# Two wide RWKV stages: VectorE's convolution taps placed behind the triangular inverse, and a new order of the filler work

## The chip, the cores and the metric

One core of one Trainium2 chip runs the whole program. The metric is device time in microseconds (us) for one execution, as the median of several runs. Engines are named as the profile names them: PE is TensorE, DVE is VectorE, ACT is ScalarE, POOL is GpSimd, SP is the queue that issues all loads.

## The reference, cut to what matters

Two blocks follow each other on 256 tokens of width 1024. The first has two layers. Each layer takes two token streams (`ctx` and `x`) through the following, cut to what the change touches:

```python
mod_x = silu_c @ ada_w[l] + ada_b[l]                      # adaLN: six shift, scale and gate rows
ux = modulate(rmsnorm(x, norm1_g[l]), sh1, sc1) @ w_in[l]  # "norm of x", then the input product
# first 1024 columns of ux: the convolution's input (value and gate); the rest: RWKV
z = val * sigmoid(gate)
z = dwconv(z, conv_w) + conv_b                             # 31 taps along the tokens, 512 channels
z = silu(group_norm(z, 8, cnorm_g, cnorm_b))
yx, s_f, s_b = rwkv_scans(prep, s0_f, s0_b)                # a recurrence over tokens in both directions
mix = concat([z, rwkv_out(yx)]);  x = x + gt1 * (mix @ w_out[l]);  then a SwiGLU
```

The second block (two layers of SwiGLU, mixer, SwiGLU) follows, and the change does not touch it.

## The kernel before, in words

Activations lie feature-major (features on the partitions, 256 tokens along the free side). A product in full precision is three matmuls of a split operand: every weight piece of 512 KB is loaded by SP into a tile `raw` (four buffers), ACT writes its high part `wh` (L341) and DVE its low part `wl` (L342), and PE runs 24 matmuls for one output of 128 features (`up`, L333 is the helper that records every matmul).

The recurrence is done in chunks of 64 tokens. For each chunk a unit triangular matrix is inverted. All of its 32x32 diagonal blocks are inverted at once by DVE: `inverse` runs 31 steps, each a multiplication (L961) and a subtraction (L963), and each step needs the one before. Beside it run `reads` (masks on DVE, L1028) and `values` (masks, L1064). Both need PE, and the inverse's result is needed by the last part, the `chain`: two groups of four steps in which small matmuls, DVE and ACT alternate. Between the chain's steps the program calls `fill(FILL)`, which takes up to six steps of a list of other work, the filler.

This arrangement, called `wide`, is used twice: for `ctx` in layer 0 (from about 100 us on) and for `x` in layer 1 (from about 1130 us on). In both its filler is the convolution's input product of the same stream (`conv_in`, 8 weight pieces) and then adaLN for four of the six rows (`ada_steps`, 32 loads of 512 KB, 16 steps). After the chain comes the depthwise convolution in program order (`conv`): of the 30 outer taps per channel group f (there are four), `NPOOL` or `NPOOLE` gives how many POOL multiplies (L731) and how many ACT multiplies (L729); POOL adds all of those products up (L732). The remaining taps and the middle one are DVE's (L718 and L725, into a tile `T1c` of two buffers), and L736 joins both sums. Products wait in `tap` tiles, of which there are two (`NTAP`).

In layer 0 the stage is followed by `conv_in` of `x`, then `w_in` of `x` (15 weight pieces), then the output product of `ctx`. The norm of `x` (`norm_x`: two loads, squares, 16 transposes L438, and 24 evictions into four tiles of the ring `S`) stands in program order after the chain. The convolution of `x` is then done by POOL alone in the background (`NPOOLC`).

The order of each engine's work is not the program's order. A planner keeps its own estimate of every instruction's cost, takes for each engine the earliest instruction in program order that is ready by that estimate, and so fills waiting time with later work. A tile must find a free buffer in its ring before its first writer is ready: `S` has 20 buffers, `z` 2, the PSUM ring `pb` 2 (the filler's products, the norm's transposes and adaLN all use `pb`). On the chip each engine then works through its list in that order. `issue_after(ins)` puts the instructions of its block behind `ins` on the same engine.

Of the kernel before, what the change touches and what calls it, by code (L numbers as in the profile page):

```python
# [12 lines left out]
ALU = mybir.AluOpType  # L13
# [21 lines left out]

NLAST = 2, 4

NPOOL, NPOOLE, NPOOLC = (14, 3), (12, 4), (30, 0)
NTAP = 2

QB, QE, QC, EVERY = (2, 3, 4, 5), (2, 3, 4, 5), (1,), 2

FILL = 6
LATER = 1500
# [214 lines left out]
class Prog:  # L259
# [440 lines left out]
    def conv(self, l, z, acc, npool, hold=False):  # L700


        nc = self.nc
        o = COLS[f"convw{l}"][0]
        taps = sorted((j for j in range(31) if j != 15), key=lambda j: abs(j - 15))
        nv, na = 30 - npool[0] - npool[1], npool[1]
        parts = [("v", taps[:nv]), ("a", taps[nv : nv + na]), ("p", taps[nv + na :])]

        order = []
        for k, js in parts:  # L710
            order += [((i + 0.5) / len(js), k, j) for i, j in enumerate(js)]
        order.sort()
        zc = [acc[:, f, :] for f in range(4)]
        for f in range(4):
            w = lambda j: self.cols[:, o + 4 * j + f : o + 4 * j + f + 1]
            av = self.T1([P, T]) if nv else None
            if nv:
                nc.vector.tensor_scalar(av, z[:, f, :], w(15), None, ALU.mult)  # L718
                nc.gpsimd.memset(zc[f], 0.0)
            else:  # L720
                nc.gpsimd.tensor_scalar(zc[f], z[:, f, :], w(15), None, ALU.mult)
            for i, (_, k, j) in enumerate(order):
                d, s = slice(max(0, 15 - j), min(T, T + 15 - j)), slice(max(0, j - 15), min(T, T + j - 15))
                if k == "v":
                    nc.vector.scalar_tensor_tensor(av[:, d], z[:, f, s], w(j), av[:, d], ALU.mult, ALU.add)  # L725
                else:
                    t = self.t(self.pool, [P, T], "tap", bufs=NTAP)
                    if k == "a":
                        nc.scalar.mul(t[:, d], z[:, f, s], w(j))  # L729
                    else:  # L730
                        nc.gpsimd.tensor_scalar(t[:, d], z[:, f, s], w(j), None, ALU.mult)  # L731
                    nc.gpsimd.tensor_add(zc[f][:, d], zc[f][:, d], t[:, d])  # L732
                if i % 5 == 4:
                    yield
            if nv:
                nc.vector.scalar_tensor_tensor(zc[f], av, self.col(f"convb{l}", f), zc[f], ALU.add, ALU.add)  # L736
            else:
                nc.gpsimd.tensor_scalar(zc[f], zc[f], self.col(f"convb{l}", f), None, ALU.add)
            yield
        while hold and not self.go:  # L740
            yield
        self.group_norm(zc, f"cng{l}", f"cnb{l}", LN_EPS, AF.Silu)
# [200 lines left out]
    def inverse(self, Ld, Lo):  # L943

        nc = self.nc
        fl = lambda t: t.rearrange("p d a c x -> p (d a c) x")
        Ld, Lo = fl(Ld), fl(Lo)  # L950
        tj = self.S([P, 32, 32])
        nc.vector.transpose(tj.rearrange("p r c -> p c r"), Ld.rearrange("p j c -> p c j"))
        X = self.S([P, 32, 32])
        nc.gpsimd.memset(X, 0.0)
        xf = X.rearrange("p r c -> p (r c)")
        nc.gpsimd.memset(xf[:, 0:1024:33], 1.0)
        for k in range(31):
            m = 31 - k
            tmp = self.T1([P, 256])
            tv = tmp[:, 0 : m * (k + 1)].rearrange("p (a b) -> p a b", b=k + 1)  # L960
            nc.vector.tensor_mul(tv, tj[:, k + 1 : 32, k : k + 1].broadcast_to([P, m, k + 1]),  # L961
                                 X[:, k : k + 1, 0 : k + 1].broadcast_to([P, m, k + 1]))
            nc.vector.tensor_sub(X[:, k + 1 : 32, 0 : k + 1], X[:, k + 1 : 32, 0 : k + 1], tv)  # L963
        yield
        qt = self.S([P, 32, 32])
        nc.vector.transpose(qt, X)
        qc = self.S([P, 32, 32])
        nc.vector.transpose(qc, X.rearrange("p r c -> p c r"))

        zss = []  # L970
        for d in range(2):
            pz = self.ps((P, 16, 32))
            zs = Lo[:, 16 * d : 16 * d + 16, :]
            for j in range(16):
                J = 16 * d + j
                for h in range(2):
                    r = slice(64 * h + 32, 64 * h + 64)
                    w = slice(64 * h, 64 * h + 32)
                    self.mm(pz[w, j, :], Lo[r, J, :], qt[r, :, J], tile_position=(64 * h + 32, 64 * h))
            for h in range(2):  # L980
                w = slice(64 * h, 64 * h + 32)
                (nc.scalar.copy if h else nc.vector.tensor_copy)(zs[w], pz[w])
            zss.append(zs)
        Q = [self.S([P, 16, CH]) for _ in range(2)]
        for d in range(2):
            nc.gpsimd.memset(Q[d], 0.0)
            js = slice(16 * d, 16 * d + 16)
            src, zs = (qt, qc)[d], zss[d]
            po = self.ps((P, 16, 32))
            for q in range(4):  # L990
                s = slice(32 * q, 32 * q + 32)
                o = (q % 2) * 32
                dst, v = Q[d][s, :, o : o + 32], src[s][:, :, js].rearrange("p c j -> p j c")
                (nc.vector.tensor_copy if q % 2 else nc.scalar.copy)(dst, v)
            for j in range(16):
                J = 16 * d + j
                for h in range(2):
                    w = slice(64 * h, 64 * h + 32)
                    r = slice(64 * h + 32, 64 * h + 64)
                    if d == 0:  # L1000
                        self.mm(po[w, j, :], qc[w, :, J], zs[w, j, :], tile_position=(64 * h, 64 * h))
                    else:
                        self.mm(po[r, j, :], zs[w, j, :], qc[w, :, J], tile_position=(64 * h, 64 * h + 32))
            for h in range(2):
                w = slice(64 * h + 32 * d, 64 * h + 32 * d + 32)
                dst = Q[d][w, :, 32 * (1 - d) : 32 * (1 - d) + 32]
                if h:
                    nc.scalar.mul(dst, po[w], -1.0)
                else:
                    nc.vector.tensor_scalar(dst, po[w], -1.0, None, ALU.mult)  # L1010
        self.Q = Q
# [399 lines left out]
    def first(self):  # L1411
        nc = self.nc
        self.setup()
        RW = list(range(NRW))
        KWV = [4, 5, 6, 7, 8, 9, 10, 11, 12]
        drain = lambda g: [None for _ in g]
# [4 lines left out]
        fl = lambda t: t.rearrange("p (a b) -> p a b", a=4)  # L1421
        z = lambda: self.t(self.pool, [P, 4, T], "z", bufs=2)

        def wide(l, x, s0, ada, perm, before=None):

            def filler():

                steps = itertools.chain(self.conv_in(l, x, fl(self.x[0])), self.ada_steps(l, ada))

                def fill(n=1):  # L1430
                    lane = self.lane
                    self.on("b")
                    for _ in range(n):
                        next(steps, None)
                    self.on(lane)

                return fill

            self.pstags = alone
            for at in self.rwkv(l, self.w_in(l, x, RW), s0, True, "wide", filler()):  # L1440
                if at == "post" and before is not None:
                    before()
            self.on("c")
            drain(self.conv(l, fl(self.x[0]), fl(self.x[1]), (NPOOL, NPOOLE)[l]))
            self.pstags = beside
            self.on("b")
            return self.mixed_in(fl(self.x[1]), self.y, perm)

        self.ada(0, (1, 0))
        cf = self.load("ctx")  # L1450
# [1 line left out]
        cf = self.norm1(0, cf, 1, False, self.xf)  # L1452
        early = []

        def norm_x():
            zt = lambda: self.t(self.pool, [P, D], "z", bufs=2)
            self.on("b")
            early.append(self.norm1(0, self.load("x", [zt(), zt()]), 0, False, self.Sr, keep=True))
            self.on("r")

        cm = wide(0, cf, None, QB, False, norm_x)
        states = self.states
        self.on("b")
        (xf,) = early
        zx = z()
        mods = self.ada_steps(0, [q for q in (2, 3, 4, 5) if q not in QB])
        for _ in self.conv_in(0, xf, zx):
            next(mods, None)
            next(mods, None)
        drain(mods)  # L1470
        win = self.w_in(0, xf, RW)
        ux = next(win)
        drain(win)
# [25 lines left out]
        for b in range(2):  # L1499
            nc.sync.dma_start(self.keep[b], self.x[b])  # L1500
        xf = self.norm1(1, self.x, 0, True, self.xf, acc=True)
        xm = wide(1, xf, states, QE, True)
        for b in range(2):
            nc.sync.dma_start(self.x[b], self.keep[b])
        f = self.out(1, self.x, 0, xm)
# [132 lines left out]
```

## Time and profile before

| | |
|---|---|
| three runs | 2772.6, 2772.72, 2775.5 us (median 2772.72) |
| the profiled execution | 2776.2 us, its span 2774.1 us |
| PE, PE weight load | busy 95% and 82% of the span |
| DVE, ACT, POOL | busy 62%, 48%, 24% |
| mean granted TensorE clock | 0.961 |

How to read it: the span runs from the first to the last instruction. PE is busy nearly always, but the granted clock, shown beside the busy time in the tables by stretch, has to be read with it: busy time at clock 0.50 does half the work of busy time at 1.00.

### The profile page before, as it was taken

The page shows a single profiled execution, that of the slowest core. Times are in us where ns is not written, and L with a number is a line of the kernel's source. Part 1 is how long each engine was busy: PE and PEld are TensorE (multiplying, and loading weights), DVE is VectorE, ACT ScalarE, POOL GpSimd, SP SyncE. Part 2 cuts the span into 40 slices and gives each one's busy share as a digit, 9 for nine tenths or more (in the row PEclk, how much of TensorE's full clock was granted, in tenths as well). Part 3 has the DMA queues.
Part 4 walks back from the last instruction along what each step waited for, and adds up shares of the span by engine and source line. Part 5 has one row for each costly group of instructions (what it writes and reads, how often), then busy time and mean ns, then how long its engine had stood idle before and what let it go on. Part 6 is the DMA issues. An engine that isn't in the chain of part 4 may idle for free.

```text
span 2774.1 us, 53770 instructions
## 1 busy us (share of the span) xinstructions
PE 2628.3 (95%) x22398; PEld 2288.3 (82%) x22398; DVE 1713.4 (62%) x2703; ACT 1327.6 (48%) x2015; POOL 667.0 (24%) x669
## 2 busy tenths in 40 slices
PE   7889988999889998899899899999999999999998
PEld 4866867888678897866799899889899898889897
DVE  3885778655577555984555655666655655755655
ACT  5533654434564346433544544654544544644543
POOL 0287999920130001384200000010000000100000
PEclk9989989999999999979899999999999999999999
DMA  7244424434323354234355555524555554525653
GB/s 251 102 153 167 153 86 167 139 129 145 137 77 115 130 181 148 100 138 153 124 188 183 198 184 188 188 86 157 183 186 186 183 186 172 170 85 183 205 185 119
DMA packets 118767, 430.70 MB, mean 155 GB/s; under 512 B 13174, under 2 KB 13686, under 8 KB 118524
## 3 DMA queue, kind: packets, MB, share of 16 engines
q1 hardware_dynamic: 118524, 427.28, 44.7%
q8 instruction: 175, 2.87, 0.4%
q14 instruction: 68, 0.56, 0.1%
HBM read 425.13 MB, written 2.10 MB: 154 GB/s over the span
## 4 chain that ended last, share of the span: by engine, by line
PE 76%; DVE 10%; POOL 5%; ACT 5%; issue 2%; DMA 2%; SPq 0%; ACTq 0%; POOLq 0%; DVEq 0%
PE pb L333 32%; PE acc L333 24%; PE ps L333 19%; POOL tap L731 3%; DVE wl L342 2%; POOL z L732 1%; DVE T1c L725 1%; DMA raw<-in_ada 1%; DVE S L963 1%; DVE T L961 1%; POOL x L732 1%; ACT wh L341 1%; PE acc L438 0%; DMA raw<-in_wr 0%; ACT L384 0%
## 5 line engine op out<-in xcount | busy, mean ns | idle before, releaser
L342 DVE TENSOR_TENSOR wl<-raw,wh 128x1024 fp32r<-128x1024 f32 (+1 forms) x654 | 814.5, 1249 | 621.6 <-ACT wh L341 390.9
L341 ACT CAST wh<-raw 128x1024 fp32r<-128x1024 f32 (+1 forms) x654 | 681.8, 1046 | 892.7 <-PE pb L333 349.8
L333 PE MATMUL pb<-xf,wh 128*128 128x256 f32 (+1 forms) x2560 | 488.1, 289 | 15.6 <-DVE T1b L588 5.2
L333 PE MATMUL pb<-S,wh 128*128 128x256 f32 x2560 | 490.9, 289 | 4.3 <-DVE S L462 1.8
L333 PEld LDWEIGHTS pb<-xf,wh 128*128 128x128 f32 (+1 forms) x2560 | 411.3, 195 | 29.7 <-DVE T1b L588 8.8
L333 PEld LDWEIGHTS pb<-S,wh 128*128 128x128 f32 x2560 | 407.7, 192 | 21.5 <-issue 11.7
L333 PE MATMUL ps<-S,wh 128*128 128x256 f32 x2048 | 390.6, 288 | 0.5 <-ACT S L460 0.4
L333 PE MATMUL pb<-xf,wl 128*128 128x256 f32 (+1 forms) x1280 | 372.8, 292 | 8.9 <-DVE wl L342 8.9
L365 POOL TENSOR_TENSOR wl<-raw,wh 128x1024 fp32r<-128x1024 f32 x22 | 52.1, 2379 | 1340.7 <-ACT wh L364 824.2
L333 PE MATMUL pb<-S,wl 128*128 128x256 f32 x1280 | 367.4, 287 | 2.1 <-DVE wl L342 2.1
L333 PEld LDWEIGHTS ps<-S,wh 128*128 128x128 f32 x2048 | 327.0, 192 | 9.4 <-issue 3.7
L333 PE MATMUL ps<-S,wl 128*128 128x256 f32 x1024 | 293.8, 287 | 0.6 <-DVE wl L342 0.6
L333 PEld LDWEIGHTS pb<-xf,wl 128*128 128x128 f32 (+1 forms) x1280 | 249.3, 195 | 16.9 <-DVE wl L342 11.7
L333 PEld LDWEIGHTS pb<-S,wl 128*128 128x128 f32 x1280 | 245.3, 192 | 7.0 <-issue 3.2
L333 PE MATMUL acc<-wh,T 128*128 128x512 f32 x704 | 206.3, 393 | 0.0
L333 PEld LDWEIGHTS ps<-S,wl 128*128 128x128 f32 x1024 | 196.7, 192 | 3.0 <-issue 1.5
L333 PE MATMUL acc<-wh,T1b 128*128 128x512 f32 x528 | 158.6, 399 | 3.5 <-ACT T1b L341 3.5
L731 POOL TENSOR_SCALAR tap<-z,cols 128x255 f32<-128x255 f32 (+14 forms) x120 | 154.4, 1295 | 0.0
L333 PEld LDWEIGHTS acc<-wh,T 128*128 128x128 f32 x704 | 127.0, 189 | 23.6
L731 POOL TENSOR_SCALAR tap<-x,cols 128x246 f32<-128x246 f32 (+6 forms) x104 | 112.9, 1093 | 46.1 <-DVE x L670 46.0
L333 PEld LDWEIGHTS acc<-wh,T1b 128*128 128x128 f32 x528 | 94.9, 190 | 22.3 <-ACT T1b L341 4.4
L333 PE MATMUL acc<-wl,T 128*128 128x512 f32 x352 | 113.3, 395 | 0.0
(445 smaller groups left out, 3956.7 us busy)
## 6 DMA issues: line engine op xcount, KB each, us to landing
raw<-in_fu SPq DMA_DIRECT2D x132, 512.0 KB, 3.2
raw<-in_ada SPq DMA_DIRECT2D x96, 512.0 KB, 4.2
raw<-in_pu SPq DMA_DIRECT2D x88, 512.0 KB, 4.3
raw<-in_qu SPq DMA_DIRECT2D x88, 512.0 KB, 4.2
raw<-in_fd SPq DMA_DIRECT2D x66, 512.0 KB, 3.2
raw<-in_wr SPq DMA_DIRECT2D x51, 512.0 KB, 3.9
raw<-in_pd SPq DMA_DIRECT2D x44, 512.0 KB, 4.3
raw<-in_qd SPq DMA_DIRECT2D x44, 512.0 KB, 4.3
```

What stands on the lines that cost most here:

```text
L333: return self.nc.tensor.matmul(out, lhsT, rhs, start=start, stop=stop, **kw)
L341: self.nc.scalar.copy(hi, src)
L342: self.nc.vector.tensor_sub(lo, src, hi.bitcast(F32))
L365: self.nc.gpsimd.tensor_sub(lo, r, hi.bitcast(F32))
L725: nc.vector.scalar_tensor_tensor(av[:, d], z[:, f, s], w(j), av[:, d], ALU.mult, ALU.add)
L731: nc.gpsimd.tensor_scalar(t[:, d], z[:, f, s], w(j), None, ALU.mult)
L732: nc.gpsimd.tensor_add(zc[f][:, d], zc[f][:, d], t[:, d])
L961: nc.vector.tensor_mul(tv, tj[:, k + 1 : 32, k : k + 1].broadcast_to([P, m, k + 1]), X[:, k : k + 1, 0 : k + 1].broadcast_to([P, m, k + 1]))
L963: nc.vector.tensor_sub(X[:, k + 1 : 32, 0 : k + 1], X[:, k + 1 : 32, 0 : k + 1], tv)
```

## The change

Three things. DVE's first instruction of each channel group's taps (L718) is put behind the last subtraction of the inverse; its other taps depend on it. In both wide stages four more taps per channel group become DVE's: layer 0 from 14 on POOL, 3 on ACT and 13 on DVE to 10, 3 and 17; layer 1 from 12, 4 and 14 to 9, 3 and 18. And in layer 0 the filler becomes: `conv_in` of `ctx`, the norm of `x`, then adaLN's steps with one `conv_in` step of `x` after every fourth; what is left is run right after the stage. In layer 1 the filler stays as it was.

```diff
-NPOOL, NPOOLE, NPOOLC = (14, 3), (12, 4), (30, 0)
+NPOOL, NPOOLE, NPOOLC = (10, 3), (9, 3), (30, 0)
...
             if nv:
-                nc.vector.tensor_scalar(av, z[:, f, :], w(15), None, ALU.mult)
+                with self.tc.issue_after(self.inverted.ins):
+                    nc.vector.tensor_scalar(av, z[:, f, :], w(15), None, ALU.mult)
                 nc.gpsimd.memset(zc[f], 0.0)
...
-            nc.vector.tensor_sub(X[:, k + 1 : 32, 0 : k + 1], X[:, k + 1 : 32, 0 : k + 1], tv)
+            self.inverted = nc.vector.tensor_sub(X[:, k + 1 : 32, 0 : k + 1], X[:, k + 1 : 32, 0 : k + 1], tv)
...
-        def wide(l, x, s0, ada, perm, before=None):
+        def wide(l, x, s0, steps, perm):
...
-                steps = itertools.chain(self.conv_in(l, x, fl(self.x[0])), self.ada_steps(l, ada))
+                all_ = itertools.chain(self.conv_in(l, x, fl(self.x[0])), steps)
...
-            for at in self.rwkv(l, self.w_in(l, x, RW), s0, True, "wide", filler()):
-                if at == "post" and before is not None:
-                    before()
+            drain(self.rwkv(l, self.w_in(l, x, RW), s0, True, "wide", filler()))
...
-        def norm_x():
+        def then_x():
+
             zt = lambda: self.t(self.pool, [P, D], "z", bufs=2)
-            self.on("b")
             early.append(self.norm1(0, self.load("x", [zt(), zt()]), 0, False, self.Sr, keep=True))
-            self.on("r")
-
-        cm = wide(0, cf, None, QB, False, norm_x)
+            yield
+            early.append(z())
+            mods, conv = self.ada_steps(0, (2, 3, 4, 5)), self.conv_in(0, *early)
+            for i, _ in enumerate(mods):
+                yield
+                if i % 4 == 1:
+                    next(conv, None)
+                    yield
+            yield from conv
+
+        steps = then_x()
+        cm = wide(0, cf, None, steps, False)
+        drain(steps)
         states = self.states
         self.on("b")
-        (xf,) = early
-        zx = z()
-        mods = self.ada_steps(0, [q for q in (2, 3, 4, 5) if q not in QB])
-        for _ in self.conv_in(0, xf, zx):
-            next(mods, None)
-            next(mods, None)
-        drain(mods)
+        xf, zx = early
...
-        xm = wide(1, xf, states, QE, True)
+        xm = wide(1, xf, states, self.ada_steps(1, (2, 3, 4, 5)), True)
```

## Rows read from the trace of the kernel before

**Rows 1.** The page: busy time by engine, and the costliest group on DVE

```profile
PE 2628.3 (95%) x22398; PEld 2288.3 (82%) x22398; DVE 1713.4 (62%) x2703; ACT 1327.6 (48%) x2015; POOL 667.0 (24%) x669
...
L342 DVE TENSOR_TENSOR wl<-raw,wh 128x1024 fp32r<-128x1024 f32 (+1 forms) x654 | 814.5, 1249 | 621.6 <-ACT wh L341 390.9
```

**Rows 2.** Stretches of both wide stages: length, busy of each engine, clock, DMA

```profile
133.00:187.40 54.40, 46.89 (x465) 32.88 (x466) 52.43 (x112) 14.29 (x25) 45.80 (x45) 0.92 0.48 165
187.40:262.00 74.60, 73.44 (x1103) 51.28 (x1101) 42.07 (x80) 28.27 (x52) 58.58 (x69) 0.83 0.47 164
262.00:310.00 48.00, 47.58 (x329) 37.48 (x330) 29.45 (x51) 28.18 (x43) 44.05 (x48) 1.00 0.29 100
1149.00:1219.90 70.90, 61.79 (x665) 46.61 (x664) 69.56 (x154) 23.12 (x39) 47.91 (x49) 0.95 0.45 157
1219.90:1283.00 63.10, 60.14 (x893) 43.32 (x891) 31.12 (x59) 20.23 (x37) 53.97 (x66) 0.73 0.42 150
1283.00:1320.00 37.00, 35.79 (x391) 24.84 (x389) 24.05 (x57) 15.79 (x27) 2.98 (x5) 0.98 0.21 75
```

**Rows 3.** The same stretches, tile T1c alone: PE, PEld, DVE, ACT busy

```profile
133.00:187.40 54.40, 0.00 (x0) 0.00 (x0) 26.10 (x43) 0.00 (x0) 0.92 0.48 165
187.40:262.00 74.60, 0.00 (x0) 0.00 (x0) 9.83 (x16) 0.00 (x0) 0.83 0.47 164
...
1149.00:1219.90 70.90, 0.00 (x0) 0.00 (x0) 26.52 (x46) 0.00 (x0) 0.95 0.45 157
1219.90:1283.00 63.10, 0.00 (x0) 0.00 (x0) 10.46 (x18) 0.00 (x0) 0.73 0.42 150
```

**Rows 4.** Chain of waits, layer 1's wide stage: start, us, what

```profile
1189.53 0.85 DVE S L963
1190.37 1.45 DVE T1c L725 x2
...
1235.30 2.15 POOL tap L731 x2
```

**Rows 5.** Who waited for whom, 1149 to 1220: us, times, longest

```profile
PE acc L333 <- DVE S L1028: 3.8, 2, 2.7
```

**Rows 6.** Ten microseconds of the chain in layer 0 and in layer 1

```profile
240.00:250.00 10.00, 10.00 (x142) 5.85 (x138) 3.31 (x8) 3.67 (x6) 5.83 (x7) 1.00 0.72 245
1240.00:1250.00 10.00, 10.00 (x153) 8.77 (x154) 5.72 (x11) 2.26 (x4) 9.60 (x13) 0.50 0.01 2
```

**Rows 7.** DVE in order of time, layer 1: two taps, and the inverse's end

```profile
1171.28 0.93 DVE L725 SCALAR_TENSOR_TENSOR T1c<-x,cols,T1c 128x254 f32<-128x254 f32 x1
...
1177.91 0.47 DVE L725 SCALAR_TENSOR_TENSOR T1c<-x,cols,T1c 128x252 f32<-128x252 f32 x1
...
1219.91 1.25 DVE L966 STREAM_TRANSPOSE S<-S 128x1024 f32<-128x1024 f32 x1
```

**Rows 8.** POOL's lines in both wide stages: duration ns min/median/max, first and last start

```profile
L731 POOL TENSOR_SCALAR tap<-x,cols x104: 888/1038/2128, 133.0 to 1277.5; 128x246 f32<-128x246 f32 x16, 128x245 f32<-128x245 f32 x16, 128x244 f32<-128x244 f32 x16, 128x243 f32<-128x243 f32 x16
L732 POOL TENSOR_TENSOR x<-x,tap x132: 691/716/1618, 134.9 to 1279.2; 128x247 f32<-128x247 f32 x16, 128x246 f32<-128x246 f32 x16, 128x245 f32<-128x245 f32 x16, 128x244 f32<-128x244 f32 x16
```

**Rows 9.** POOL in order of time, layer 0: the last addition of the convolution

```profile
275.78 0.70 POOL L732 TENSOR_TENSOR x<-x,tap 128x241 f32<-128x241 f32 x1
```

**Rows 10.** Chain of waits, layer 0: one weight piece of conv_in of x

```profile
264.52 3.07 PE pb L333 x24
```

**Rows 11.** SP's queue, layer 0: start, us from first to last issue

```profile
138.54 99.96 SPq L348 DMA_DIRECT2D raw<-in_ada  x32
```

**Rows 12.** Ten microseconds after layer 0's wide stage, columns as in Rows 2

```profile
390.00:400.00 10.00, 4.62 (x49) 3.91 (x49) 9.64 (x13) 5.40 (x10) 10.00 (x6) 0.68 0.31 107
```

**Rows 13.** DVE in order of time, layer 0: the last mask of values

```profile
217.62 0.41 DVE L1064 TENSOR_TENSOR T<-acc,const 64x256 f32<-64x256 f32 x1
```

**Rows 14.** PE in order of time, layer 0: adaLN, and the norm's first transposes

```profile
181.42 1.05 PE L333 MATMUL pb<-raw,csil 128*32 128x512 f32 x4
...
251.02 0.64 PE L438 MATMUL pb<-const,z 128*128 128x128 f32 x4
```

More of the change, by code (lines that the diff above doesn't have):

```diff
@@ L36 @@
 NLAST = 2, 4
-NPOOL, NPOOLE, NPOOLC = (14, 3), (12, 4), (30, 0)
+NPOOL, NPOOLE, NPOOLC = (10, 3), (9, 3), (30, 0)
 NTAP = 2
-QB, QE, QC, EVERY = (2, 3, 4, 5), (2, 3, 4, 5), (1,), 2
+QC, EVERY = (1,), 2
 FILL = 6
@@ L1433, in fill @@
                     for _ in range(n):
-                        next(steps, None)
+                        next(all_, None)
                     self.on(lane)
```

## The prediction

> **What bounds the kernel now.** I read the page first. PE is busy 95% of the span [rows 1], so a change on another engine can only win where PE waits or works slowly. Next come the two wide stages cut into stretches, inverse, chain and tail [rows 2]. The reader should multiply PE's busy time by the granted clock. Layer 1: 61.79 × 0.95 + 60.14 × 0.73 + 35.79 × 0.98 = 137.7 us of work at full clock in 171.0 us, so 33.3 us are lost. Layer 0: 46.89 × 0.92 + 73.44 × 0.83 + 47.58 × 1.00 = 151.7 in 177.0, lost 25.3. No gain in these stretches can be larger than that.
>
> Who holds PE back shows in the same table. While the inverse runs, DVE is busy 52.43 of 54.40 us and 69.56 of 70.90 [rows 2]. In the chain's stretches it is busy only 42.07 of 74.60 and 31.12 of 63.10. The taps alone take 26.10 us (43 instructions) and 26.52 us (46) before the inverse is done, and 9.83 and 10.46 behind it [rows 3]. The chain of waits runs through this pattern, an inverse step and then two taps [rows 4], and PE waits there for masks from DVE [rows 5]. After the inverse the chain passes to POOL's taps [rows 4]. What low clock costs shows in two tens of microseconds, both with PE "busy" 10.00: with adaLN's matmuls between the chain's the clock was 1.00, with next to no loads (DMA share 0.01) it was 0.50, the lower of its two levels [rows 6].
>
> **The change part by part.**
>
> *Taps behind the inverse.* The inverse ended at 1219.9 in layer 1 [rows 7] and at 187.4 in layer 0, where the stretches are cut. Without the taps' 26.1 and 26.5 us it would end at 161.3 and 1193.4, since DVE's other work there (52.43 − 26.10 = 26.3 us; 69.56 − 26.52 = 43.0 us) is what remains [rows 2, 3]. That is 52.6 us on DVE, not on the kernel. PE had only 7.5 and 9.1 us idle in these stretches [rows 2]; the rest of what it can win is the clock of the chain's stretch, if adaLN's matmuls now fall between the chain's steps instead of before them.
>
> *Four more taps per group on DVE.* There are 4 × (1 + 17 + 1) = 76 tap instructions in layer 0 and 80 in layer 1, against 60 and 64. The mean one took 35.93 / 59 = 0.609 us and 36.98 / 64 = 0.578 us [rows 3]. So 16 more cost 9.7 and 9.2 us of DVE, and all taps together 46.3 and 46.2 us, now all behind the inverse. Does DVE have room? Layer 1: if the stage ended when it does now, the stretch behind the inverse would be 63.1 + 26.5 = 89.6 us, and DVE's work in it 31.12 − 10.46 + 46.2 = 66.9. The stage can come forward by 22.7 us before DVE is full. Layer 0: 74.6 + 26.1 = 100.7 us against 42.07 − 9.83 + 46.3 = 78.5, plus what the filler brings in: eight splits at 1.25 [rows 1] and small work, say 11. That leaves 11 us.
>
> *Fewer taps on POOL.* Layer 0 loses 16 multiplies and 16 additions, 16 × 1.038 + 16 × 0.716 = 28.1 us at the medians; layer 1 loses 12 and 16 (four of the additions were of ACT's products), 23.9 us [rows 8]. POOL's part ran from 133.0 to 276.5 in layer 0 and to 1280 in layer 1 [rows 8, 9]; where the chain of waits goes over POOL behind the inverse [rows 4], the convolution would end some 24 us sooner. ACT's four multiplies fewer lie beside its 20 of 63 busy us [rows 2]; I cost them at nothing.
>
> *The filler's order, layer 0.* What moves: the norm's two loads, squares, 16 transposes and 24 evictions, to ahead of adaLN; and `conv_in` of `x`, eight loads of 512 KB, eight splits on ACT and DVE, 192 matmuls, four sigmoids and products, in among adaLN's 32 loads on SP's queue. A weight piece takes PE 3.07 us [rows 10], 24.6 us for eight. This is no work saved; it moves out of the tail and into the chain's stretch, and `w_in` of `x` must cover the tail's group norms in its place. The eight loads pass 32 that took 100 us to issue [rows 11] at a DMA share of 0.47, where 0.72 was reached with 245 GB/s [rows 2, 6]: 4.2 MB at that rate are 17 us of 75 that stand half empty, so nothing for the loads, and 17 us if that room is gone. The norm's share on POOL and DVE is in the 11 us above.
>
> *What follows layer 0.* POOL's background convolution of `x` starts earlier. At 390 to 400 POOL is full and PE works 4.62 of 10 us [rows 12]. I expect POOL still full there, so nothing; the bounds are the 5.4 us that PE idles, either way.
>
> *The sum.* Layer 1: bounds 0 and 33.3 (PE), 23.9 (POOL), 22.7 (DVE); a list ordered by estimated costs won't reach the tightest, and I take two thirds of it, −15. Layer 0: bounds 0, 25.3 (PE) and 28.1 (POOL); DVE's 11 us limit the chain but not the tail, which loses `conv_in`; I take about half of PE's, −12. Together −27 us. The profiled execution had a span of 2774.1 us and 2.1 around it, 2776.2 in all, which is 3.5 above the median of the runs; it would become 2749, and the median 2772.7 − 27 = 2746.
>
> **The rivals.** *DVE becomes the bound behind the inverse (slower).* A tap took 0.47 us or 0.93 us, within seven microseconds of each other, with POOL at work [rows 7]. If all taps behind the inverse pay 0.93, DVE needs 31.12 − 10.46 + 80 × 0.93 = 95.1 us in layer 1 where 89.6 are there (+5.5), and 42.07 − 9.83 + 11 + 76 × 0.93 = 113.9 in layer 0 where 100.7 are there (+13.2). That is 2772.7 + 18.7 = 2791. It decides from a mean tap of 69/80 = 0.86 us in layer 1 and 57.5/76 = 0.76 in layer 0. For it: POOL still runs beside the chain, and a chain step queues behind whole taps on DVE. Against it: the mean over all taps was 0.59, with POOL busy 45.8 of 54.4 us beside them [rows 2, 3]. The Trainium skill, SBUF — State Buffer, section "Who interferes with whom", says that a VectorE instruction with two SBUF inputs (a tap has two) and a GpSimd instruction that reads SBUF exclude each other for a whole instruction; by that rule taken strictly this rival would hold as long as POOL runs. The trace agrees in part: 0.93 beside 0.47, but a mean far nearer to the latter.
>
> *The norm blocks the filler (smaller gain).* By the code the ring `S` is full with 20 tiles while reads and values run, until the last mask of values, at 217.6 before [rows 13]. The norm needs four of them, and its transposes hold the two `pb` buffers that adaLN uses too. In the old order the transposes came behind adaLN, at 251.0, and adaLN's matmuls covered PE while the inverse ran, as at 181.4 [rows 14]. Ahead of adaLN the norm could shut it out until `S` has room. Layer 0's 12 us are then gone and layer 1's stay: 2758.
>
> *Nothing comes out.* PE's list gets a similar mixture, the chain still runs at low clock, and the time returns as waits inside the chain: within 5.5 us of 2772.7. For it: PE idled only 7.5 and 9.1 us beside the inverse.
>
> *Near the floors.* The clock stays up through both chains: −33.3 − 25.3 gives 2714 at the least, say 2726 for most of this case.
>
> **How the numbers follow.** My forecast, 2735 to 2758, has 0.45. Near the floors, 2714 to 2735, 0.10. The blocked filler, 2758 to 2767, 0.15. Within 0.2% (5.5 us, about what runs of this kernel can tell from no change, their spread being 2.9 us) 0.13. DVE as the bound, above 2778, 0.17. So faster 0.70, same 0.13, slower 0.17. The range 2726 to 2778 holds 0.45 + 0.15 + 0.13 and 0.07 of the case near the floors, 0.80.
>
> **What would show it.** Right if: no T1c instruction stands before the inverse's end, and the inverse takes about 44 us from 1149 instead of 71; the mean tap stays below 0.76 us; the granted clock in the chain's stretch rises above 0.83 and 0.73; POOL's part shortens by 28 us from 143 in layer 0, and by 24 in layer 1; and `conv_in` of `x` is through by the chain's end. Wrong if the taps cost 0.9 us, if the chain's DVE instructions start late behind taps, if adaLN's first matmul comes only behind the norm's transposes with PE idle before it, or if PE's gaps turn up again in the tail because the group norms have no cover.

## The result, and the profile after

The changed kernel takes 2792.37 us (median of five, 2787.57 to 2795.86) beside 2772.72 before: a ratio of 1.0061 [1.0045, 1.0077], slower by 0.6%. The forecast was 2746, its range 2726 to 2778. The profiled execution has a span of 2794.1 us and a mean granted clock of 0.950, where before had 2774.1 and 0.961; each of the two profiled executions lies 3.5 us above its kernel's median.

The page of after: busy time by engine. It looks like [rows 1], with 53 us fewer on POOL.

```profile
PE 2640.2 (94%) x22398; PEld 2307.3 (83%) x22398; DVE 1728.3 (62%) x2735; ACT 1318.7 (47%) x2007; POOL 613.7 (22%) x609
```

For the comparison I cut both wide stages into four stretches, at five events: the inverse's first and last instruction, the chain's first and last write of a state, and the next stage's first load (`in_fu`). The kernel before first, layer 0 and then layer 1; columns as in [rows 2].

```profile
113.40:187.40 74.00, 63.15 (x654) 47.70 (x653) 67.64 (x154) 27.27 (x47) 45.80 (x45) 0.89 0.44 150
187.40:222.20 34.80, 34.80 (x501) 25.14 (x501) 22.35 (x37) 12.34 (x19) 29.40 (x34) 0.64 0.25 89
222.20:268.70 46.50, 44.91 (x690) 31.92 (x685) 23.57 (x50) 18.19 (x37) 35.72 (x42) 1.00 0.56 196
268.70:367.80 99.10, 98.65 (x653) 84.04 (x652) 66.83 (x101) 59.39 (x91) 94.45 (x95) 1.00 0.44 150
...
1149.70:1219.90 70.20, 61.09 (x659) 45.93 (x657) 68.86 (x152) 22.95 (x39) 47.91 (x49) 0.95 0.45 158
1219.90:1260.10 40.20, 40.20 (x607) 31.68 (x607) 24.28 (x42) 15.19 (x26) 34.99 (x42) 0.62 0.27 94
1260.10:1298.80 38.70, 35.74 (x600) 25.11 (x597) 18.07 (x44) 11.31 (x22) 18.98 (x25) 0.96 0.61 218
1298.80:1336.30 37.50, 35.68 (x131) 22.34 (x130) 20.48 (x42) 16.53 (x29) 9.70 (x12) 0.86 0.08 29
```

The changed kernel, cut at the same events:

```profile
113.70:164.00 50.30, 40.35 (x477) 37.25 (x475) 44.80 (x99) 22.12 (x38) 29.48 (x32) 0.91 0.28 96
164.00:208.50 44.50, 36.52 (x519) 30.53 (x519) 40.95 (x77) 18.26 (x30) 37.40 (x37) 0.58 0.20 72
208.50:296.70 88.20, 85.61 (x976) 63.08 (x976) 42.02 (x89) 21.57 (x43) 72.66 (x82) 0.88 0.55 195
296.70:382.30 85.60, 84.42 (x526) 70.34 (x525) 57.09 (x94) 48.77 (x80) 80.68 (x82) 0.96 0.43 152
...
1163.70:1208.20 44.50, 40.91 (x491) 34.53 (x489) 42.34 (x92) 16.80 (x28) 27.99 (x29) 1.00 0.38 134
1208.20:1267.60 59.40, 48.32 (x608) 34.79 (x609) 58.45 (x112) 17.47 (x30) 53.06 (x57) 0.63 0.33 123
1267.60:1318.00 50.40, 49.95 (x763) 34.11 (x762) 20.80 (x52) 12.96 (x25) 1.42 (x2) 0.90 0.55 200
1318.00:1353.20 35.20, 34.65 (x131) 21.58 (x130) 20.64 (x42) 16.51 (x29) 10.02 (x12) 0.90 0.08 26
```

The inverse does take 50.3 and 44.5 us instead of 74.0 and 70.2. The next stretch, from its end to the chain's first step, grows from 34.8 to 44.5 and from 40.2 to 59.4, and there DVE is now busy 40.95 of 44.50 and 58.45 of 59.40 us. The chain grows from 46.5 to 88.2 and from 38.7 to 50.4.

The taps by themselves, tile T1c as in [rows 3]:

```profile
113.40:163.90 50.50, 0.00 (x0) 0.00 (x0) 0.00 (x0) 0.00 (x0) 0.91 0.28 95
163.90:230.00 66.10, 0.00 (x0) 0.00 (x0) 38.98 (x75) 0.00 (x0) 0.60 0.22 81
1163.30:1208.20 44.90, 0.00 (x0) 0.00 (x0) 0.07 (x1) 0.00 (x0) 1.00 0.37 133
1208.20:1267.00 58.80, 0.00 (x0) 0.00 (x0) 44.51 (x79) 0.00 (x0) 0.63 0.34 124
```

None before the inverse's end (the 0.07 us of one stand on the edge of the cut); 0.52 and 0.56 us for the mean tap behind it. Where they stand in DVE's list is seen in order of time, layer 1. In the changed kernel L726 are the taps (L725 before) and L1065 the values' masks (L1064 before):

```profile
1245.17 6.80 DVE L726 SCALAR_TENSOR_TENSOR T1c<-x,cols,T1c 128x255 f32<-128x255 f32 x11
...
1255.23 4.49 DVE L726 SCALAR_TENSOR_TENSOR T1c<-x,cols,T1c 128x250 f32<-128x250 f32 x7
1259.65 0.41 DVE L1065 TENSOR_TENSOR T<-acc,const 64x256 f32<-64x256 f32 x1
```

and on PE, which stands still for that mask (in brackets the wait ahead of the instruction, and for what):

```profile
1260.11 0.68 PE L333 MATMUL acc<-S,S 64*64 64x64 f32 x8 [4.12 <-DVE T L1065]
...
1266.58 1.65 PE L333 MATMUL acc<-xf,T 64*64 64x64 f32 x26 [2.59 <-DVE T L1065]
```

At the end of layer 0's wide stage the changed kernel is 14.5 us late (382.3 against 367.8). By the last load of `in_fd` ahead of layer 1's wide stage (1059.17 against 1046.47) it is 12.7 late, at the end of that stage 16.9, at the end of the span 20.0. So layer 0's wide stage costs 14.5 us, layer 1's (from that load on) 4.2, and stages that nobody edited -1.8 and +3.1.

The last view is SP's queue in layer 1, before and then after: start, us, how many loads.

```profile
1170.23 89.03 SPq L348 DMA_DIRECT2D raw<-in_ada  x25
...
1263.41 9.91 SPq L348 DMA_DIRECT2D raw<-in_ada  x7
```

```profile
1183.36 73.09 SPq L348 DMA_DIRECT2D raw<-in_ada  x20
...
1277.24 16.42 SPq L348 DMA_DIRECT2D raw<-in_ada  x12
```

Before, 25 of the 32 adaLN loads were issued ahead of the chain; now 20, and 12 fall into it.

### The profile page after: what moved, and what is told of

It is laid out like the page before. It is cut to its first block, busy times and chain, and to the rows that moved or that the text cites. A ratio compares the mean times of both kernels' runs of the same rounds, so it can differ in the third digit from the quotient of the medians.

```text
span 2794.1 us, 53718 instructions
## 1 busy us (share of the span) xinstructions
PE 2640.2 (94%) x22398; PEld 2307.3 (83%) x22398; DVE 1728.3 (62%) x2735; ACT 1318.7 (47%) x2007; POOL 613.7 (22%) x609
## 4 chain that ended last, share of the span: by engine, by line
PE 78%; DVE 13%; ACT 4%; issue 2%; DMA 2%; POOL 1%; SPq 0%; ACTq 0%; DVEq 0%; POOLq 0%
PE pb L333 33%; PE acc L333 24%; PE ps L333 19%; DVE wl L342 2%; DVE T1c L726 2%; DVE S L964 1%; DVE T L962 1%; DMA raw<-in_ada 1%; ACT wh L341 1%; POOL tap L732 1%; DVE acc L619 0%; PE acc L438 0%; DVE x L620 0%; DMA raw<-in_wr 0%; DVE S L851 0%
## 5 line engine op out<-in xcount | busy, mean ns | idle before, releaser
L333 PEld LDWEIGHTS pb<-S,wh 128*128 128x128 f32 x2560 | 413.4, 194 | 22.0 <-issue 9.8
L732 POOL TENSOR_SCALAR tap<-z,cols 128x255 f32<-128x255 f32 (+14 forms) x120 | 138.2, 1161 | 0.0
L733 POOL TENSOR_TENSOR z<-z,tap 128x255 f32<-128x255 f32 (+14 forms) x120 | 110.4, 920 | 4.1
```

The lines of the kernel that those rows point to most:

```text
L333: return self.nc.tensor.matmul(out, lhsT, rhs, start=start, stop=stop, **kw)
```

## The experiments

Theory A: all taps, released together at the inverse's end, stand in DVE's list ahead of the transposes, copies and masks that the chain needs. Its rivals: B, layer 0's filler costs; C, the four more taps cost; D, what the inverse had covered (filler, adaLN's loads) now lengthens the chain; E, the lower clock itself is the cause. Every ratio is to the kernel before on the same chip.

### The three parts

`e1` is the tie alone, `e2` the shares alone, `e3` layer 0's filler alone, `e4` tie and shares with the old filler.

```diff
# e1 and e4
+                with self.tc.issue_after(self.inverted.ins):
# e2 and e4
+NPOOL, NPOOLE, NPOOLC = (10, 3), (9, 3), (30, 0)
# e3
+        steps = then_x()
```

> The kernel before with the tie alone: 60 and 64 of the 76 and 80 taps, each f's first one held until the inverse ends; the shares of the engines and layer 0's filler as before. Theory A (order: taps released together at the inverse's end stand in VectorE's list ahead of the transposes, the copies to Q and the values' masks, and the four more make that list longer): the inverses end at some 164 and 1195 us as after the change, but the first step of the chain gains less than 12 us of the 24, and the time is 2768 to 2782 us, about even with before. Theory B (layer 0's filler is what costs, by the norm that holds two banks and the ring S; the tie by itself is the gain forecast): layer 1 comes out 10 or more shorter and layer 0 too, 2745 to 2755 us. Theory C (the 16 more taps a layer, 16 x 0.55 = 9 us a layer, are the loss and the tie is neutral): 2772 us.

> The kernel before with the four more taps alone (shares 10, 3 and 9, 3 for GpSimd and ScalarE), nothing tied, layer 0's filler as before. Theory A (order behind the inverse): the 16 more taps a layer fall in part beside the inverse at the blocked 0.93 us or so, which makes its end 5 to 8 us later, and GpSimd's adds end earlier: 2770 to 2783 us. Theory B (layer 0's filler): 2765 to 2775 us. Theory C (the four more are the loss): 2772 + 2 x 9 = 2790 us, near to the changed kernel's 2792.

> The kernel before with layer 0's new filler alone (norm of x first, then adaLN in turns with the convolution's input product), no tie, the old shares. Theory A (order behind the inverse): 2765 to 2776 us, since the convolution's input product of x moves from behind into the chain's holes and the norm's blocking costs about as much. Theory B (the filler costs): layer 0 loses the 14 us that the changed kernel shows at the first load of its output product, 2783 to 2790 us, while layer 1 is as before.

> The changed kernel with layer 0's filler put back to that of before: the tie and the four more taps stay. Theory A (order behind the inverse): VectorE is full behind both inverses as in the changed kernel, and the time stays at 2785 to 2795 us. Theory B (the filler costs): layer 0's 14 us come back, layer 1 keeps its 6: 2776 to 2780 us. Theory C (the four more taps): as A.

| kernel | median us | ratio |
|---|---|---|
| e1, tie | 2793.94 | 1.0073 [1.0058, 1.0088] |
| e2, four more | 2778.5 | 1.0007 [0.9998, 1.0016] |
| e3, filler | 2808.69 | 1.0118 [1.0104, 1.0132] |
| e4, tie and four more | 2807.65 | 1.0113 [1.0097, 1.0129] |

Only `e2` came out in a stated range, A's; `e1`, `e3` and `e4` lie above all of theirs. By themselves the four more taps cost nothing that can be measured; behind the tie they cost 14 us (`e4` against `e1`), where C had 18 in either case. The tie alone costs as much as the whole change, and the filler alone more. The parts don't add up: with tie and four in place, the kernel with the new filler is some 14 us faster (the changed kernel against `e4`). No theory had foreseen that. But the 14 us are not gained where the filler was edited: layer 0's stage ends at 381.7 in `e4` and at 382.3 in the changed kernel. They lie in layer 1, whose code is the same in both. Layer 1 of `e4`:

```profile
1158.70:1203.00 44.30, 38.95 (x479) 33.34 (x477) 42.18 (x92) 16.26 (x27) 26.46 (x27) 1.00 0.33 111
1203.00:1267.30 64.30, 51.40 (x612) 38.43 (x615) 58.29 (x111) 17.99 (x31) 50.75 (x54) 0.54 0.18 65
1267.30:1327.60 60.30, 56.46 (x771) 36.18 (x763) 20.63 (x54) 12.65 (x24) 3.80 (x5) 0.90 0.66 236
1327.60:1365.40 37.80, 35.84 (x131) 22.48 (x130) 20.53 (x43) 16.57 (x29) 9.74 (x12) 0.86 0.07 25
```

Its four stretches take 206.7 us, those of the changed kernel 189.5; in `e4` 20 adaLN loads fall into the chain instead of 12. The planner had written another order for the same stage. In `e3` layer 0's wide stage is 18.5 us late; the norm, ahead of adaLN, leaves SP four adaLN loads from 141.74 on and eight more strung over 174 to 238, as rival two of the prediction had it. But layer 1 of `e3`, whose code is that of before, loses another 14.3 us, again in another order (22 adaLN loads are issued ahead of its chain, not 25).

### DVE's order behind the inverse

`e5` ties the taps to DVE's last copy to Q, `e6` to its last mask of `values`, `e7` leaves out DVE's taps.

```diff
# e5
-            self.inverted = nc.vector.tensor_sub(X[:, k + 1 : 32, 0 : k + 1], X[:, k + 1 : 32, 0 : k + 1], tv)
+                    self.inverted = nc.vector.tensor_scalar(dst, po[w], -1.0, None, ALU.mult)
# e6
+                    self.inverted = nc.vector.tensor_mul(ga[:, h], pg[h],
# e7
-                    nc.vector.scalar_tensor_tensor(av[:, d], z[:, f, s], w(j), av[:, d], ALU.mult, ALU.add)
+                    pass
```

> The changed kernel with each f's first tap held until VectorE's last copy to Q instead of the inverse's end, so that the two transposes and VectorE's copies to Q stand ahead of all taps. Theory A (taps stand ahead of the critical work in VectorE's list, and TensorE's waits for it let the clock fall): the first step of the chain comes some 10 us earlier after the inverse's start in both layers and the time falls to 2770 to 2782 us. Theory D (the stretch is set by the filler that is left over: every adaLN load that comes behind the chain's first step makes the chain 1.6 us longer, and the time at the lower granted clock grows with the stretch in which TensorE has no dense work): Q earlier or not, the time stays at 2788 to 2798 us, with 120 to 135 us lost to the clock.

> The changed kernel with each f's first tap held until the last of the values' masks on VectorE. Theory A: no mask waits for a tap any more, TensorE's waits for masks go, and the time is 2765 to 2780 us, unless the taps then run on beside the chain and hold GpSimd's adds. Theory D: 2788 to 2800 us; the chain comes earlier, but the adaLN loads left to it grow from 12 to 16 or more in layer 1 and the chain is longer by 1.6 us for each.

> The changed kernel without VectorE's taps in the two wide layers: the convolution leaves out 18 and 17 of its 30 side taps of each f; the first scaling, the tie and the join stay, as do GpSimd's and ScalarE's taps. VectorE is then almost free behind the inverse. Theory A: the 20 us of the loss come back and more, 2750 to 2770 us, and the time lost to the clock is at or below the 108.7 us of before. Theory D: VectorE free or not, the filler is spent or left over, the time lost to the clock stays above 120 us, and the time is 2780 to 2792 us.

`e5`: 2807.77 us, 1.0110 [1.0094, 1.0126]. `e6`: 2793.02, 1.0056 [1.0044, 1.0068]. `e7`: 2772.29, 0.9987 [0.9978, 0.9996].

`e5` lies above both ranges. Its chain starts 7.9 and 4.3 us earlier after the inverse's start than in the changed kernel, where A had some 10, and then takes longer (90.6 and 62.8 us instead of 88.2 and 50.4).

`e6` is the telling one. The stages of `e6`, cut at the same events:

```profile
112.50:162.50 50.00, 40.34 (x477) 37.23 (x477) 44.87 (x99) 22.15 (x38) 29.50 (x32) 0.91 0.29 96
162.50:196.40 33.90, 33.83 (x505) 28.42 (x503) 18.91 (x31) 17.78 (x28) 26.50 (x30) 0.60 0.27 95
196.40:289.60 93.20, 84.74 (x1011) 62.45 (x1009) 71.44 (x138) 23.18 (x45) 81.33 (x89) 0.94 0.56 197
289.60:370.80 81.20, 80.04 (x500) 65.41 (x500) 55.70 (x92) 48.02 (x79) 74.94 (x78) 1.00 0.44 146
...
1152.70:1196.50 43.80, 38.35 (x479) 33.08 (x477) 42.38 (x92) 16.54 (x27) 26.78 (x27) 1.00 0.35 112
1196.50:1236.50 40.00, 39.06 (x607) 31.81 (x609) 17.79 (x34) 17.29 (x29) 34.67 (x43) 0.66 0.22 79
1236.50:1308.30 71.80, 58.74 (x768) 36.23 (x765) 50.41 (x128) 12.55 (x24) 20.02 (x17) 0.86 0.59 212
1308.30:1347.50 39.20, 37.26 (x138) 23.48 (x137) 22.59 (x49) 17.81 (x32) 7.62 (x12) 0.87 0.10 29
```

With the masks first, the stretch between inverse and chain is back at 33.9 and 40.0 us, as before: A is right for that stretch, and the chain's first step comes 26.6 us earlier after the inverse's start in layer 1 (83.8 us instead of the 110.4 of the kernel before), the whole of what the inverse gave. And layer 1 is none the shorter: its chain now takes 71.8 us instead of 38.7. DVE's taps run beside it, and PE waits for the chain's own additions (in all, times, longest):

```profile
PE acc L333 <- DVE T L1094: 8.9, 2, 8.5
```

while 20 adaLN loads are left to it:

```profile
1173.13 61.38 SPq L348 DMA_DIRECT2D raw<-in_ada  x12
...
1242.09 32.22 SPq L348 DMA_DIRECT2D raw<-in_ada  x12
...
1280.97 11.03 SPq L348 DMA_DIRECT2D raw<-in_ada  x8
```

For the whole kernel D's range held (2788 to 2800), A's did not (2765 to 2780): with the masks first the time is nearly that of the changed kernel, 1.0056 beside 1.0061.

`e7` says what the taps cost the changed kernel, 20 us, and that even without DVE's taps the change is worth only 0.1%. A had said 2750 to 2770, D 2780 to 2792; it lies between. With the taps gone, DVE waits for PE in the stretch between layer 1's inverse and chain, for the products that it is to mask:

```profile
DVE T L1065 <- PE acc L333: 24.4, 11, 6.0
```

In `e6` that wait is 11.1 us, in the changed kernel 0.6.

### The filler earlier, and fewer loads

`e8` writes out 14 of layer 1's 20 filler steps ahead of the rest of the inverse, in the changed kernel; `e11` does it in both wide layers of the kernel before; `e12` in both layers together with the masks' tie, the four more taps and the old filler. `e9` (on `e6`), `e10` (on before) and `e13` (on `e7`) load one adaLN tile in four.

```diff
# e8, e11 and e12
+        if wide:
+            fill(14)
         for _ in inv:
# e9, e10 and e13
+                        if l == 0 or q < 2 or k4 + k2 == 0:
                             r = self.raw(f"ada{l}", nb * 4 + k4 * 2 + k2)
```

In `e8` the condition is `wide and l == 1`; in `e13` it lacks `l == 0`, so both layers load less.

> The changed kernel with 14 of layer 1's 20 filler steps written out ahead of the rest of the inverse (transposes, copies to Q), and so with precedence over it, instead of with the chain; layer 0 as in the changed kernel. Theory D: fewer adaLN loads are left to layer 1's chain (4 or less in place of 12), the chain is some 13 us shorter, dense products of TensorE stand in the stretch in which the clock is 0.50, and the time falls by 5 to 12 us to 2780 to 2787 us. Theory A: VectorE is as full as before and the chain comes later by what the filler takes: 2790 to 2797 us.

> The kernel before with 14 of the 20 filler steps of each wide layer written out ahead of the rest of the inverse. There 25 of 32 loads of layer 1, and nearly all of layer 0, come ahead of the chain already, so by theory D little changes: 2768 to 2776 us, the chain's start later by what its length loses. If the filler's place is a gain by itself, 2760 to 2768 us.

> The tie behind the values' masks, four more taps, layer 0's filler as before, and 14 of the 20 filler steps of each wide layer ahead of the rest of the inverse: VectorE's order mended and the filler spent early at the same time. Theory D: with 4 or fewer adaLN loads left to it the chain of layer 1 is some 25 us shorter than the 72 us of the tie behind the masks and starts 10 to 20 us later, so 2770 to 2783 us; only if the early filler fits beside VectorE's masks without holding them does it come below before, 2755 to 2770 us. Theory A: 2760 to 2775 us.

> The kernel whose taps are tied behind the values' masks (2793 us), with only 8 of layer 1's 32 adaLN weight loads made; the products take each loaded tile four times, so the modulation of layer 1 is not the reference's. TensorE has the same products. Theory D1 (the transfers of the adaLN tiles that are left to the chain set its length, 1.6 us each): layer 1's chain falls from 72 to 30 to 45 us and the time by 20 to 35 us, to 2758 to 2773. Theory D2 (the products and the order of the left filler on TensorE, at the lower clock, set it): the chain stays at 60 to 72 us and the time at 2785 to 2793.

> The kernel before with the same cut of layer 1's adaLN loads to 8 of 32. Only 7 loads stand in its chain. Theory D1: 7 x 1.6 = 11 us at most, 2762 to 2770 us. Theory D2: 2770 to 2777 us.

> The changed kernel without VectorE's taps in the two wide layers (they are left out of the convolution, as in the run without taps, 2772 us) and with only 8 of 32 adaLN weight loads in each of those layers (each tile is taken four times, so the modulations are not the reference's). If the earlier inverse was eaten by the two things that it had been covering, taps and adaLN loads, then with both gone its 25 us come out in each wide layer: layer 1's stretch from the inverse's start to the chain's last step is 125 us or less instead of 149, and the time is 2715 to 2740 us. If TensorE itself, at the granted clock of the stretch, is what binds behind the inverse (theory E: span times mean clock is about 2665 us in every kernel here), the stretch stays above 138 us and the time at 2750 to 2768.

| kernel | median us | ratio |
|---|---|---|
| e8, changed, filler early in layer 1 | 2781.17 | 1.0025 [1.0013, 1.0038] |
| e11, before, filler early | 2777.78 | 1.0016 [1.0005, 1.0028] |
| e12, masks' tie, filler early | 2790.88 | 1.0056 [1.0041, 1.0071] |
| e9, masks' tie, a quarter of the loads | 2772.53 | 0.9992 [0.9982, 1.0001] |
| e10, before, a quarter of the loads | 2770.01 | 0.9978 [0.9969, 0.9987] |
| e13, no DVE taps, a quarter of the loads | 2754.06 | 0.9919 [0.9903, 0.9936] |

D gains: the same cut of loads is worth 18 to 20 us in `e6` and 5 to 6 in the kernel before, whose chain has 7 of them and not 20. But `e9`'s chain takes 57.4 us in layer 1, where D1 had 30 to 45: the loads are only a part of it. `e8` gives the changed kernel 10 us back, as D said, with 4 adaLN loads left to the chain. Where the 10 us lie its profile can't show, since that execution took 2789.82 us, 8.7 above the median. `e11` came out just above its ranges. `e12` missed A's range and D's: PE is busy 48.12 us in a chain of 61.9, with the taps beside it as in `e6`. With taps and loads both gone, `e13` gains 22 us, where the theory that these two had eaten the gain wanted 35 to 60; theory E's 2750 to 2768 holds, and so does its bound on the stretch (over 138 us; it took 140.9). Its layer 1:

```profile
1142.00:1187.00 45.00, 39.06 (x480) 33.38 (x477) 42.47 (x92) 16.81 (x28) 27.97 (x29) 0.99 0.31 107
1187.00:1234.00 47.00, 44.99 (x606) 33.65 (x607) 20.51 (x39) 16.80 (x30) 35.69 (x45) 0.64 0.08 24
1234.00:1282.90 48.90, 47.00 (x774) 32.49 (x773) 20.40 (x55) 13.66 (x27) 10.42 (x14) 0.97 0.29 99
```

DVE is free (20.5 of 47 us), the loads are gone (DMA share 0.08), and PE is busy throughout: 774 matmuls in the chain, where the kernel before had 600, for it had done the others beside its longer inverse.

### The clock, and the order by itself

`e14` and `e15` add 20 products to each wide layer's `values`, in the kernel before and in the changed one; `e16` and `e17` set `FILL` to 5 and 7 in the kernel before.

```diff
# e14 and e15
+        self.mm(out, self.const[:, 0:n], self.const[:, 0 : out.shape[1]])
# e16; e17 has 7
-FILL = 6
+FILL = 5
```

> The kernel before with 20 products added to each wide layer's values: one of 256 or 512 columns into each bank of the masks' products and of the readout just ahead of the real ones, which write over it. At 0.29 us a 256 columns they are some 7 us of TensorE a layer at the full clock. If the lower clock is a cause (theory E), denser work in the stretch at 0.50 lifts the mean clock, the time lost to it falls from 108.7 us to 90 to 100, and the time is 2760 to 2775 us in spite of the added work. If it only marks waits (theory D), the added work is added: 2778 to 2795 us.

> The changed kernel with the same 20 added products in each wide layer. Theory E: the 129 us lost to the clock fall to 105 to 118 and the time is 2770 to 2787 us. Theory D: 2793 to 2810 us.

> The kernel before with five filler steps in place of six behind each step of the chain: the same instructions in another order on every engine (VectorE's list differs in 1019 lines of 2646, most of them by names and places). If the order that comes out of such a nudge is worth up to 10 us a wide layer, as the runs with unedited stages suggest, the time is anywhere from 2765 to 2795 us; if orders are nearly equal, 2772 to 2780.

> The kernel before with seven filler steps in place of six behind each step of the chain, a smaller nudge of the order. By either theory as the run with five: 2765 to 2795 us if orders count, 2772 to 2780 if not.

`e14`: 2803.05 us, 1.0103 [1.0083, 1.0122], above both ranges. `e15`: 2794.41, 1.0069 [1.0050, 1.0089], in D's. The added products were mis-sized: PE is busy 17.2 us a layer with them, not 7. The kernel before pays 27 us for these 34; the changed kernel pays about 2. In the changed kernel the time lost to the lower clock (span times one minus the mean clock) falls from 129 to 111 us, and span times clock rises by about as much. Layer 1's four stretches even take 184.7 us instead of 189.5, with more products in them. The second stretch, from the inverse's end to the chain's start:

```profile
1215.80:1268.40 52.60, 50.20 (x612) 31.09 (x612) 43.59 (x92) 16.43 (x28) 37.73 (x40) 0.84 0.29 102
```

Its clock is 0.84 instead of 0.63. But DVE is busy 43.59 us in it instead of 58.45, so the order has changed too. The changed kernel thus had room on PE. Whether the clock is a cause of its own these two don't settle; it is not the only one, since `e12` loses 104.6 us to the lower clock, less than the kernel before with 107.3 on the same chip, and is still 0.56% slower.

`e16`: 2785.85 us, 1.0030 [1.0017, 1.0043]. `e17`: 2776.37, 1.0003 [0.9991, 1.0014]. The same instructions in another order are worth some 9 us in the one case and nothing in the other.

No kernel with the whole computation is faster than the one before. All that have the tie and all taps (`e1`, `e4`, `e5`, `e6`, `e8`, `e12`, `e15` and the changed kernel) are slower, by 0.25% to 1.13%.

## Why the prediction was wrong

Take from each stretch PE's busy time times the clock, as the prediction did, and what is left is lost to PE. In us, from the rows above and the same cuts of `e1`, `e3`, `e4`, `e7` and `e13`:

| | beside the inverse | to the chain | chain | tail | sum |
|---|---|---|---|---|---|
| layer 0, before | 17.8 | 12.5 | 1.6 | 0.5 | 32.4 |
| after | 13.6 | 23.3 | 12.9 | 4.6 | 54.4 |
| e1, tie alone | 8.8 | 17.6 | 15.8 | 0.9 | 43.2 |
| e4, tie and four | 10.6 | 25.1 | 12.2 | 4.1 | 52.0 |
| e6, taps behind the masks | 13.3 | 13.6 | 13.5 | 1.2 | 41.6 |
| e7, no taps on DVE | 13.5 | 12.7 | 5.2 | 1.5 | 32.9 |
| layer 1, before | 12.2 | 15.3 | 4.4 | 6.8 | 38.7 |
| after | 3.6 | 29.0 | 5.4 | 4.0 | 42.0 |
| e1 | 3.6 | 24.1 | 10.5 | 3.8 | 42.0 |
| e4 | 5.3 | 36.5 | 9.5 | 7.0 | 58.4 |
| e6 | 5.4 | 14.2 | 21.3 | 6.8 | 47.7 |
| e7 | 5.3 | 22.8 | 7.7 | 5.9 | 41.7 |
| e3, code as before | 17.3 | 19.1 | 12.4 | 7.4 | 56.2 |
| e13 | 6.3 | 18.2 | 3.3 | 5.8 | 33.6 |

PE's work in layer 1 is the same before and after, 147.9 and 147.5 us at full clock. It was 58.0 of that beside the inverse before and 40.9 after; of the 17.1 taken away there, 5.5 come back in the next stretch and 10.7 in the chain.

Two steps failed, and `e7` tells them apart. The forecast was -27 us. With DVE's taps left out the same change is worth 0.13%, some 4 us; with them it loses some 17, by the ratio. So about half of the miss lies in the gain, which was not there even with free taps (the losses of `e7` in the table sum to 32.9 and 41.7 us, none smaller than before), and about half in the taps' cost, 20 us that the prediction put at nothing. No run leaves the taps out of the kernel before, so what they cost beside the inverse is not known, and order alone moves such times by some 9 us.

*The inverse's term.* 161.3 and 1149 + 44 were forecast for its end; it ended at 164.0 and took 44.5 us. Right. But the step from DVE to the kernel failed. The prediction said that PE had only 7.5 and 9.1 us idle beside the inverse and that "the rest of what it can win is the clock of the chain's stretch". The first half was the whole of it: what PE lost beside the inverse fell by 4.2 and 8.6 us (in `e1`, with the old filler, by 9.0 and 8.6), and the bounds of 25.3 and 33.3, of which -12 and -15 were taken, counted losses behind the inverse that its earlier end doesn't touch. The stretch to the chain takes 33 to 35 us in layer 0 and 40 in layer 1, at a clock of 0.60 to 0.66, with the inverse late (before) or early (`e6`). In layer 1 of `e7` and `e13` it is longer, 52.9 and 47.0 us without any tap: there DVE waits 24.4 and 16.8 us for PE's products, 11.1 in `e6`. Why PE's list is slower there, I have not found. `e13`, with taps and loads gone, is 9.8 us shorter in layer 1; 5 of these are losses, and the rest is PE's work, which comes out at 143.1 us instead of 147.9 though its products are the same.

*DVE's room.* This is the step whose failure made the sign. The sum was 66.9 us of DVE's work in 89.6 and 78.5 in 100.7, the verdict that the stage "can come forward by 22.7 us before DVE is full", and the taps' price held, 0.52 and 0.56 us against 0.609 and 0.578. But a list is not a sum: the masks at 1259.65 stood behind 11 and then 7 taps, while PE waited. The prediction had this among its signs of being wrong ("if the chain's DVE instructions start late behind taps"), but no term of its sum priced it. The loss to the chain's start rose by 10.8 and 13.7 us; `e6`, which changes only what the taps stand behind, takes it back to 13.6 and 14.2. In layer 0 that is a gain of 11.5 us (the stage ends at 370.8 instead of 382.3). In layer 1 the loss turns up in the chain, 15.9 us more than after. So the order explains where the taps cost, not that they cost: 46 us of taps must stand somewhere, and in all three places tried behind the inverse (the changed kernel, `e5`, `e6`) the kernel is slower. That they held up little that PE needed soon as long as they stood beside the inverse is my reading; `e2`, where 16 more cost 0.07%, agrees.

*Four more taps, POOL, the filler.* POOL's part did shorten as forecast. The last addition of layer 0's convolution (L733, L732 before) starts at 243.2, 275.8 before [rows 9]:

```profile
L733 POOL TENSOR_TENSOR x<-x,tap x52: 684/740/2055, 135.4 to 243.2; 128x245 f32<-128x245 f32 x8, 128x244 f32<-128x244 f32 x8, 128x243 f32<-128x243 f32 x8, 128x246 f32<-128x246 f32 x8
```

No run shows a gain from it: the shares alone (`e2`) are at 1.0007. `conv_in` of `x` went through by the chain's end, as written; with the filler the chain had to carry it and 20 adaLN loads from 233 on, which is part of the 88.2 us. The clock of the whole stretch from the inverse's end to the chain's end did not rise: 0.78 and 0.75, where the same stretch before had 0.84 and 0.78 (0.83 and 0.73 in the prediction's cut). It is 0.58 and 0.63 up to the chain's first step and 0.88 and 0.90 after it.

*The rivals.* DVE as the bound gave 2791. That this is the measured time within 2 us is luck: the place was right, DVE behind the inverse, but the mechanism another. It wanted a mean tap of 0.76 and 0.86 us, and got 0.52 and 0.56 with POOL busy 54.21 of 66.10 us beside it. The rule of the Trainium skill (SBUF — State Buffer, section "Who interferes with whom"), taken strictly, is thus not borne out by this mean. "Nothing comes out", time that returns behind the inverse at a low clock, is what `e7` shows once the taps are gone. The norm that blocks the filler was real in layer 0 when it came alone (`e3`, 25.0 us lost beside the inverse instead of 17.8) and cost little once the tie was there (`e4` loses 52.0 us in that layer, the changed kernel 54.4).

What stays open: how layer 0's 14.5 us split between taps, filler and order. `e16` and layer 1 of `e3` move by 9 and 14 us, and layer 1 of `e4` by 17, with unedited code in another order, so no difference of single stages is good to better than some 10 us.

## What to carry to other kernels

Before shortening something that the profile shows as long, add up what the bound engine loses beside it: expect no more than that, whatever its length, and see that the rest of the cover moves into what follows. Work released together ahead of a latency chain takes its place in an in-order list by the planner's estimate, so check for room by position (what stands ahead of each mask), not by sum. And nudge the order of the kernel before: a change whose gain is no larger than that (9 us here) can't be told from its order.

## What the runs showed of the hardware

Span times mean clock was nearly a constant over kernels that differ by 33 us: 2665.4 before, 2668.6, 2668.4 and 2669.5 in `e1`, `e2` and `e3`, 2660.1 after (means of 4 to 16 runs), while the time lost to the lower clock went from 108 to 138. Runs of one kernel differ the same way: `e1` had spans from 2785.8 at 0.958 to 2802.3 at 0.952. It is no law: with a quarter of the loads it was 2653.5 (`e10`) and 2644.4 (`e13`), and in `e12` 2683.4. In `e6` PE's clock was 0.66 over 40 us in which it counted as busy 39.06, with 607 small matmuls: a busy PE and a fast one are two things.
